# One number in a hybrid SSD and forgetting-attention layer: the last group's recurrence enters the stream of products one product later

## The chip, the cores and the metric

The kernel runs on one core of a Trainium2 chip. The metric is the device time of one execution in microseconds (us), given as the median of several runs. The core has five engines with a queue each: TensorE (PE in the profile, with its weight loads as PEld), VectorE (DVE), ScalarE (ACT), GpSimd (POOL) and SyncE (SP), which here only issues DMAs.

## The reference

One decoder layer over a sequence of 1024 tokens with 1024 channels, all in float32. A Mamba-2 branch (SSD) and a forgetting-attention branch share one input projection and are merged by gates:

```python
h = rmsnorm(x)
z_ssm, xbc, dt, q, k, v, f, z_att, g_ssm, g_att = split(h @ w_in)
xs, B, C = split(silu(causal_conv(xbc)))           # 16 heads of 64, 4 groups, state 128
dt = softplus(dt + dt_bias);  a = -exp(a_log)
# chunks of 128 tokens: inside a chunk  y = ((C B^T) * decay) (xs dt), between chunks a carried state
y_ssm = group_rmsnorm(ssd(xs, dt, a, B, C, d_skip) * silu(z_ssm))
# 16 attention heads of 64, logits q.k/8 + F[t] - F[s], F = cumsum(log sigmoid(f)), causal
y_att = attention(q, k, v, f) * silu(z_att)
merged = sigmoid(g_ssm) * (y_ssm @ w_branch_ssm) + sigmoid(g_att) * (y_att @ w_branch_att)
out = x + rmsnorm(merged @ w_out)
```

## The kernel before, in words

**Products.** All large projections are computed as pairs: two blocks of weight columns against the input, by a scheme of seven products of half-sized blocks instead of eight. A product has one operand made from the input (`x0` to `x6`, each split into a high part `x0h` and a low part `x0l`) and one made from the weights (`wop`, from a loaded piece `raw` or a `sum` of pieces). It is 12 matmuls of 128x512 (the helper in line 130), and it is run in two halves of 6. The weight operands are split by ScalarE (L354, the high part) and VectorE (L356, the low part; L363 and L379 make the sums). Products accumulate in the PSUM banks `pb`, `pc`, `pd`; VectorE and ScalarE take them out (L410, L418, L420, L422, L424), and what follows a finished projection (a tanh in L668, a product in L669, a store) stands right behind.

**The stream.** `Stream` holds one long list of products: for each of the four SSM groups first the pairs b and c, q, x, z, v, k; then the gates (`za`, `gs`, `ga`); then the two branch projections and the last one. `half()` runs the next half of a product, with the preparation of the third product behind it, and one entry of `chores` (small pieces of other work, such as those of `weights_work`, L243 and L244). `until(pair)` runs on to the end of a pair, and `beside(gen)` runs a generator that yields how many halves are to be run between its pieces. So the order of everything is written out: TensorE, and with it the other engines, meet the pieces of the recurrence and of the attention at fixed places among the products.

**The SSM part.** For each group: when its x pair is done, some halves run, and then the recurrence `ssd(g)` beside the stream: 8 chunks of 128 tokens. The conv of x (L803) and its SiLU (L810 on ScalarE, L811 on VectorE, which makes `xs`) come before. Per chunk: `sums` loads the cumulated decays, broadcast to all partitions (`csb`, L859, on SP's queue); `decays` makes the decay matrix `m` from them on ScalarE (L891 four times, L895); `first` turns `xs` and `bt` on TensorE into the bank `tr` (L133) and makes there the product of `ct` and `bt`; out of `tr` come `xdt` (L872, VectorE), `cbm` (L877, VectorE), `bn` (L880, ScalarE) and the masked `m` (L882, VectorE). `more` makes `xe` on GpSimd, `states` the matmul `st` from `bn` and `xe`, `second` the outputs `yps` from `m` and `xdt`. Its norm (`gate_and_norm`) runs beside the stream ahead of the next group's recurrence, after the last group ahead of the attention.

**The attention part.** Eight pairs of heads with six sets of scores each run beside the remaining products. A set is: `scores` (matmuls into four banks `s`, a custom sum and row minimum in L1526 on VectorE, the exponential in L1530 on ScalarE, both into `ex`), `turned` (TensorE turns `ex` into banks `pt`, which share the four buffers of `s`; ScalarE, and VectorE in L1548 for one bank of up to four, copy them to `p`), `weighted` (the matmul `av`). When a pair of heads has two of its six sets done, its row factors are settled (L1425, L1427, L1439 to L1444, VectorE), turned, stored by GpSimd's DMA (`st_dram`, L1454) and read back broadcast to all partitions as `rb` by SP's DMA (L1460); L1491 on VectorE multiplies the outputs by `rb`. `fill` shares the products that are left over all these pieces, with fixed weights.

## Time and profile before

| What | Value |
|---|---|
| median of 3 runs | 1295.31 us (1292.98 to 1297.67) |
| the profiled execution | 1294.79 us, of which the span is 1293.1 us |
| TensorE's granted clock, mean over the span | 0.997 |
| TensorE (PE) busy | 1253.8 us, 97%, 7066 instructions |
| its weight loads (PEld) | 986.1 us, 76%, beside the matmuls |
| VectorE (DVE) busy | 1014.7 us, 78% |
| ScalarE (ACT) busy | 794.3 us, 61% |
| GpSimd (POOL) busy | 284.6 us, 22% |
| DMA | 233.60 MB, HBM 182 GB/s over the span |

A row of the profile's timeline has the start in us from the span's start, the duration in us, the engine, the line, the operation, what is written from what, the shapes, and in square brackets the idle time ahead of it and what ended it. "128x512" is 128 partitions by 512 elements; `PE s L130 <- DVE p L1548` reads: TensorE's matmul into `s` waited for what VectorE did to `p` in line 1548. A row of a stretch has its window, its length, then for TensorE, its weight loads, VectorE, ScalarE and GpSimd the busy time with the count of instructions, TensorE's granted clock, and the DMA's share and GB/s.

### The profile page before, as it was taken

What the parts mean: (1) busy time and instruction counts of PE and PEld (TensorE: products, weight loads), DVE (VectorE), ACT (ScalarE), POOL (GpSimd) and SP (SyncE); (2) the same over time, 40 slices, a digit from 0 to 9 for tenths busy, and PEclk for the clock granted to TensorE, in tenths of its full rate; (3) what the DMA queues carried; (4) which work ended last, traced back from release to release, by engine and by line L of the source; (5) the groups of instructions that cost most, each with busy time, mean ns of one, the idle gap of its engine ahead of it and who ended that gap; (6) DMA issues with size and microseconds to landing.
All of it is one profiled execution on the core that took longest, in us unless ns stands there. A gap on an engine that the chain in (4) does not pass through costs nothing. (4 is left out here: it accounts for less than half of the span.)

```text
span 1293.1 us, 21078 instructions
## 1 busy us (share of the span) xinstructions
PE 1253.8 (97%) x7066; PEld 986.1 (76%) x7066; DVE 1014.7 (78%) x1979; ACT 794.3 (61%) x1728; POOL 284.6 (22%) x307
## 2 busy tenths in 40 slices
PE   6999999999999999899999999999999999999998
PEld 4787888788888888688776777777767777678786
DVE  6998888888789878788676766676789767876875
ACT  8755666466556756566555666566677556743654
POOL 0000330024102320143001222222121313256052
PEclk9999999999999999999999999999999999999999
DMA  7332543644363545445564657666677657665932
GB/s 281 104 106 71 154 148 121 199 140 146 127 210 116 153 153 164 122 154 154 168 237 153 221 175 224 193 208 196 228 282 250 219 178 253 230 219 189 364 112 102
DMA packets 154669, 233.60 MB, mean 181 GB/s; under 512 B 17216, under 2 KB 62656, under 8 KB 154560
## 3 DMA queue, kind: packets, MB, share of 16 engines
q1 hardware_dynamic: 142016, 205.53, 49.8%
q0 software_dynamic: 6400, 16.10, 3.3%
q10 hardware_dynamic: 6144, 10.62, 2.2%
q8 instruction: 56, 0.92, 0.3%
q14 instruction: 53, 0.43, 0.1%
HBM read 162.99 MB, written 72.34 MB: 182 GB/s over the span
## 5 line engine op out<-in xcount | busy, mean ns | idle before, releaser
L356 DVE TENSOR_TENSOR wop<-sum,wop 128x512 fp32r<-128x512 f32 x174 | 140.5, 808 | 53.4 <-ACT wop L354 52.7
L354 ACT ACTIVATE wop<-sum 128x512 fp32r<-128x512 f32 x174 | 108.8, 626 | 99.0 <-DVE sum L363 44.7
L1530 ACT ACTIVATE ex<-ex,nm 128x512 f32<-128x512 f32 (+1 forms) x192 | 116.1, 606 | 76.9 <-DVE nm L1526 75.7
L410 ACT ACTIVATE s<-pb 128x512 f32<-128x512 f32 x141 | 83.5, 592 | 97.3 <-PE pb L130 95.9
L130 PE MATMUL pc<-x3h,wop 128*128 128x512 f32 x384 | 131.6, 399 | 2.5 <-ACT wop L354 2.0
L130 PE MATMUL pb<-x0h,wop 128*128 128x512 f32 x384 | 132.2, 400 | 0.7 <-ACT x0h L1246 0.6
L130 PE MATMUL pc<-x2h,wop 128*128 128x512 f32 x384 | 131.4, 399 | 0.4 <-DVE u L422 0.4
L130 PE MATMUL pb<-x6h,wop 128*128 128x512 f32 x376 | 129.2, 399 | 1.6 <-ACT s L410 1.6
L130 PE MATMUL pb<-x5h,wop 128*128 128x512 f32 x376 | 128.3, 398 | 1.3 <-ACT s L410 1.3
L130 PE MATMUL pb<-x4h,wop 128*128 128x512 f32 x376 | 128.6, 398 | 0.2 <-DVE wop L356 0.2
L356 DVE TENSOR_TENSOR wop<-raw,wop 128x512 fp32r<-128x512 f32 x149 | 104.3, 702 | 29.8 <-ACT wop L354 29.5
L1526 DVE CUSTOM_DVE_ANT_0 ex<-s,fb 128x512 f32<-128x512 f32 (+1 forms) x192 | 96.8, 553 | 24.4 <-PE s L130 24.3
L354 ACT ACTIVATE wop<-raw 128x512 fp32r<-128x512 f32 x151 | 93.8, 623 | 15.8 <-PE pc L130 10.1
L130 PE MATMUL pd<-x1h,wop 128*128 128x512 f32 x264 | 89.1, 396 | 0.0
L130 PEld LDWEIGHTS pc<-x3h,wop 128*128 128x128 f32 x384 | 72.1, 188 | 20.2 <-issue 3.8
L130 PEld LDWEIGHTS pb<-x0h,wop 128*128 128x128 f32 x384 | 72.5, 189 | 17.2 <-ACT x0h L1246 1.3
L130 PEld LDWEIGHTS pc<-x2h,wop 128*128 128x128 f32 x384 | 72.1, 188 | 16.1 <-DVE u L422 0.8
L130 PEld LDWEIGHTS pb<-x6h,wop 128*128 128x128 f32 x376 | 70.6, 188 | 18.1 <-ACT s L410 2.7
L130 PEld LDWEIGHTS pb<-x5h,wop 128*128 128x128 f32 x376 | 70.6, 188 | 17.5 <-ACT s L410 2.2
L130 PEld LDWEIGHTS pb<-x4h,wop 128*128 128x128 f32 x376 | 70.5, 188 | 15.7 <-issue 0.7
L130 PE MATMUL s<-k,q 64*128 64x512 f32 (+3 forms) x576 | 75.7, 373 | 6.2 <-DVE p L1548 4.4
L214 POOL TENSOR_TENSOR wd<-wd 128x256 f32<-128x256 f32 x32 | 31.3, 978 | 228.3 <-DMA wd<-in_wo 125.7
(341 smaller groups left out, 3012.1 us busy)
## 6 DMA issues: line engine op xcount, KB each, us to landing
raw<-in_wu SPq DMA_DIRECT2D x128, 256.0 KB, 3.7
csb<-cs_dram SPq DMA_DIRECT2D x32, 256.0 KB, 5.5
fb<-f_dram SPq DMA_DIRECT2D x16, 512.0 KB, 6.5
rb<-st_dram SPq DMA_DIRECT2D x48, 128.0 KB, 3.2
wd<-in_wo SPq DMA_DIRECT2D x40, 128.0 KB, 3.1
xt<-in_x SPq DMA_DIRECT2D x8, 512.0 KB, 5.8
gs_dram<-th ACTq DMA_DIRECT2D x16, 256.0 KB, 3.4
qh_dram<-th SPq DMA_DIRECT2D x16, 256.0 KB, 5.2
```

The source lines that it names most:

```text
L130: return tc.keep_in_program_order(nc.tensor.matmul(*args, **kw))
L214: pin(nc.gpsimd.tensor_tensor(t[out_], t[a_], t[b_], ALU.subtract))
L354: nc.scalar.activation(op[:, 0], src, AF.Copy, scale=sign)
L356: nc.vector.tensor_tensor(op[:, 1], src, op[:, 0], ALU.subtract)
L410: nc.scalar.activation(s, ps, AF.Copy)
L1526: nc.vector.tensor_tensor_reduce(o, s[e][:, 0:w], fb[hp, h][:, e, 0:w], 1.0, 3.0e38, ALU.add, ALU.min, nm)
L1530: pin(nc.scalar.activation(o, o, AF.Exp, scale=-1.0, bias=nm, accum_out=hd.at(hd.sm, i, h, e)))
```

## The change

```diff
@@ the loop over the four SSM groups
             stream.beside(norm)
             stream.until(by_group[g][2])
-            stream.halves(4)
+            stream.halves(4 if g < 3 else 6)
             if g == 0:
                 stream.chores += list(weights_work())
             stream.beside(ssd(g))
             norm = gate_and_norm(g)
```

Between the end of the x pair of group 3 and its recurrence three products stand instead of two. The instructions are the same in number on every engine; the order is the same up to this place. Behind it all pieces of the last recurrence, of its norm and of the attention up to the last pair of heads stand one product later among the products. The pieces of the last pair of heads have two halves of products less between them, since the list of products ends where it did.

TensorE, where the last group's recurrence begins (`tr` is the bank into which the first chunk is turned, `pb<-x5h` the end of the last product of pair z, `pb<-x0h` the first product of pair v, `pb<-x6h` the second). Before:

```order
L130 MATMUL pb<-x5h,wop 128x512
L133 MATMUL tr<-ident,xs_5243 128x128
L133 MATMUL tr<-ident,xs_5350 128x128
L133 MATMUL tr<-ident,bt 128x128
L130 MATMUL tr<-ct,bt 128x128
L130 MATMUL pb<-x0h,wop 128x512
```

Now:

```order
L130 MATMUL pb<-x0h,wop 128x512
L133 MATMUL tr<-ident,xs_5243 128x128
L133 MATMUL tr<-ident,xs_5350 128x128
L133 MATMUL tr<-ident,bt 128x128
L130 MATMUL tr<-ct,bt 128x128
L130 MATMUL pb<-x6h,wop 128x512
```

The whole product of `x0` (12 matmuls) now stands ahead of the turning instead of behind it.

ScalarE at the same place, from the tanh of the SiLU (L810) to the copy of `bn` and the decay matrices (`m_5514` is that of the second chunk, whose first has been made further up; `m_5492` is that of the first). Before:

```order
L810 ACTIVATE th<-xs_5243 128x512
L410 ACTIVATE s<-pb 128x512
L354 ACTIVATE wop<-raw 128x512
L668 ACTIVATE th<-th 128x512
L880 ACTIVATE bn<-tr 128x128
L891 ACTIVATE m_5514<-csb,cscol 128x128 x4
L668 ACTIVATE th<-th 128x512
```

Now:

```order
L810 ACTIVATE th<-xs_5243 128x512
L410 ACTIVATE s<-pb 128x512
L354 ACTIVATE wop<-raw 128x512
L668 ACTIVATE th<-th 128x512 x2
L410 ACTIVATE s<-pb 128x512
L243 ACTIVATE wl<-wd 128x256
L891 ACTIVATE m_5492<-csb,cscol 128x128 x4
L354 ACTIVATE wop<-sum 128x512
L880 ACTIVATE bn<-tr 128x128
```

`bn` stood behind one tanh of L668; it now stands behind both, an L410, an L243, the four L891 of the first chunk and an L354.

VectorE at the same place, from the SiLU to `xdt` and `cbm`. Before:

```order
L811 SCALAR_TENSOR_TENSOR xs_5350<-th,xs_5350 128x512 x2
L420 TENSOR_TENSOR th<-pd,s 128x512
L356 TENSOR_TENSOR wop<-sum,wop 128x512
L811 SCALAR_TENSOR_TENSOR xs_5243<-th,xs_5243 128x512
L872 TENSOR_TENSOR xdt<-tr,dtn 128x256
L877 TENSOR_TENSOR cbm<-tr,tri 128x128
L422 TENSOR_TENSOR th<-pc,s 128x512
```

Now:

```order
L811 SCALAR_TENSOR_TENSOR xs_5350<-th,xs_5350 128x512 x2
L356 TENSOR_TENSOR wop<-sum,wop 128x512
L420 TENSOR_TENSOR th<-pd,s 128x512
L811 SCALAR_TENSOR_TENSOR xs_5243<-th,xs_5243 128x512
L363 TENSOR_TENSOR sum<-sum,raw 128x512
L422 TENSOR_TENSOR th<-pc,s 128x512
L356 TENSOR_TENSOR wop<-raw,wop 128x512
L669 SCALAR_TENSOR_TENSOR th<-th 128x512
L872 TENSOR_TENSOR xdt<-tr,dtn 128x256
L877 TENSOR_TENSOR cbm<-tr,tri 128x128
```

Four operations for the products (`sum`, L422, `wop`, L669) now stand ahead of `xdt` and `cbm`.

VectorE in the first pair of heads, behind the multiplication by `rb` (L1491, two rows ahead of the first one here), up to the copy of `p`. Before:

```order
L1427 TENSOR_TENSOR dd<-nr,nm 128x4 x2
L422 TENSOR_TENSOR th<-pc,s 128x512
L356 TENSOR_TENSOR wop<-sum,wop 128x512
L1439 TENSOR_TENSOR sm<-sm,dd 128x8
L379 TENSOR_TENSOR sum<-sum,raw 128x512
L669 SCALAR_TENSOR_TENSOR th<-th 128x512
L1440 TENSOR_TENSOR sm<-sm 128x4
L1441 RECIPROCAL sm<-sm 128x4
L1444 SCALAR_TENSOR_TENSOR ns<-dd,sm 128x8
L1548 COPY p<-pt 128x512
```

Now:

```order
L1427 TENSOR_TENSOR dd<-nr,nm 128x4 x2
L356 TENSOR_TENSOR wop<-raw,wop 128x512
L1439 TENSOR_TENSOR sm<-sm,dd 128x8
L1440 TENSOR_TENSOR sm<-sm 128x4
L1441 RECIPROCAL sm<-sm 128x4
L1444 SCALAR_TENSOR_TENSOR ns<-dd,sm 128x8
L1548 COPY p<-pt 128x512
```

Three operations of 128x512 (L422, L379, L669) no longer stand between L1491 and the copy of `p`.

On SP's queue the third load of `csb` stood ahead of the second of two loads of `raw`, a store of `t_w`, two stores of the gate z (`zg_dram`, L670) and a store of `t_low`; it now stands behind them.

## The prediction: what the later entry does to the time

> **What bounds the kernel now.** I read the page's busy times first, then TensorE's waits by line, then the timelines of TensorE, VectorE and ScalarE around the last group's entry, and then the same three engines wherever TensorE waited long in the attention part behind it.

> ```profile
> PE 1253.8 (97%) x7066; PEld 986.1 (76%) x7066; DVE 1014.7 (78%) x1979; ACT 794.3 (61%) x1728; POOL 284.6 (22%) x307
> ...
> PE s L130 <- DVE p L1548: 4.4, 4, 3.2
> PE tr L133 <- DVE xs L811: 2.5, 1, 2.5
> PE pc L130 <- ACT wop L354: 2.0, 1, 2.0
> ```

> TensorE is the bound: busy 97% of the span, and its instructions are the same 7066 after the change, in another order. So the time moves only by TensorE's waits, and by any change of its clock. Three long ones count here: 3.2 us before a set of scores (`s`), 2.5 us before the turning (`tr`) of the values, 2.0 us before a product into `pc`. The second is the one the change touches. It is in the last group:

> ```profile
> 540.53 0.39 PE L130 MATMUL pb<-x5h,wop 128*128 128x512 f32 x1
> 540.76 0.27 PE L133 MATMUL tr<-ident,xs 128*128 128x128 f32 x1
> 543.54 0.33 PE L133 MATMUL tr<-ident,xs 128*128 128x128 f32 x1 [2.51 <-DVE xs L811]
> ...
> 543.96 0.48 PE L130 MATMUL pb<-x0h,wop 128*128 128x512 f32 x1
> ...
> 548.14 0.59 PE L130 MATMUL st<-xe,bn 128*128 128x256 f32 x2
> ...
> 550.06 0.66 PE L130 MATMUL yps<-m,xdt 128*64 128x128 f32 x8
> ...
> 1148.98 2.72 PE pb L130 x12
> ```

> TensorE stands at the turning from 540.76 to 543.54, because VectorE has not finished the SiLU (L811). From there to the `st` and `yps` of the first chunk it runs without a wait. A whole product of twelve matmuls takes 2.72 us, a half 1.36 us.

> **The change part by part: the turning's wait.** Nothing is added or removed. The recurrence and the norm of group 3 (8 chunks with their matmuls, their VectorE, ScalarE and GpSimd work, 8 `csb` loads and the loads and stores of the norm on SP's queue) stand one product later. The product `pb<-x0` now runs at 540.76, where its weights are ready (it started without a wait at 543.96, and its operand was made from a `raw` piece ahead of the SiLU). It ends at 543.48; the turning is released at 543.54. So the 2.5 us of waiting are filled: **-2.5 us**. The 2.0 us wait into `pc` (535 us) lies ahead of the place where the orders part and stays.

> **What is late next.** VectorE does not get faster by this: TensorE merely arrives earlier at the next results.

> ```profile
> 542.27 1.82 DVE L811 SCALAR_TENSOR_TENSOR xs<-th,xs 128x512 f32<-128x512 f32 x2
> 544.01 0.68 DVE L420 TENSOR_TENSOR th<-pd,s 128x512 f32<-128x512 f32 x1
> 544.61 0.68 DVE L356 TENSOR_TENSOR wop<-sum,wop 128x512 fp32r<-128x512 f32 x1
> 545.21 0.68 DVE L811 SCALAR_TENSOR_TENSOR xs<-th,xs 128x512 f32<-128x512 f32 x1
> 545.81 0.41 DVE L872 TENSOR_TENSOR xdt<-tr,dtn 128x256 f32<-128x256 f32 x1
> ...
> 546.34 0.68 DVE L422 TENSOR_TENSOR th<-pc,s 128x512 f32<-128x512 f32 x1
> ...
> 548.75 0.68 DVE L882 TENSOR_TENSOR m<-m,cbm 128x512 f32<-128x512 f32 x1
> ```
> ```profile
> 546.52 0.28 ACT L880 ACTIVATE bn<-tr 128x128 f32<-128x128 f32 x1 [1.10 <-DVE cbm L877]
> 546.69 1.27 ACT L891 ACTIVATE m<-csb,cscol 128x128 f32<-128x128 f32 x4
> 547.87 0.62 ACT L668 ACTIVATE th<-th 128x512 f32<-128x512 f32 x1
> 548.39 0.40 ACT L243 ACTIVATE wl<-wd 128x256 fp32r<-128x256 f32 x1
> 548.69 0.58 ACT L410 ACTIVATE s<-pb 128x512 f32<-128x512 f32 x1
> 549.17 0.62 ACT L354 ACTIVATE wop<-sum 128x512 fp32r<-128x512 f32 x1
> 549.69 0.62 ACT L895 ACTIVATE m<-m 128x512 f32<-128x512 f32 x1
> ...
> csb<-cs_dram SPq DMA_DIRECT2D x32, 256.0 KB, 5.5
> ```

> I walk through the new order with these starts (on VectorE a 512-wide operation each 0.60 us: 544.01, 544.61, 545.21). VectorE, free of the two SiLU operations at 544.01, does `wop`, `th` (L420), the third SiLU, `sum`, and then L422, which runs 546.41 to 547.09. TensorE: turning 543.54 to 543.96, product `pb<-x6` to 546.68, and then `pc<-x2`, which adds onto the bank that L422 reads: it waits 0.4 us. After half a product (548.45) comes `st`, which needs `bn`. On ScalarE `bn` now stands behind the second L668, which needs L422's result: 547.1 + 0.52 (L668) + 0.48 (L410) + 0.30 (L243) + 1.18 (four L891) + 0.52 (L354) = 550.1, and 0.28 for `bn` itself: `st` starts at 550.4, **a wait of 1.9 us**. Behind it half a product and `st` end at 552.0. `yps` needs `m`: four more L891 (551.4), L895 (552.0), then L882 on VectorE (552.7): 0.7 us. Together 0.4 + 1.9 + 0.7 = **+3.0 us** where no wait stood before. So the local sum is +0.5 us: the wait changes its place. Bounds: -2.5 us if none of the three appears (before the change none did), and +2 us, since the third `csb` load now stands on SP's queue behind stores that wait for VectorE until about 550 us; with 5.5 us to landing it comes at about 555.5, and its four L891 (558.09 before) then end just in time for the next `st`; a late landing would add about 1.5 us. GpSimd's `xe` only follows `xdt`, ahead of `bn`, and is not what `st` waits for.

> **The attention part.** It keeps its halves between the pieces up to the last head, but each piece meets other products. The longest wait of all lies in the first head:

> ```profile
> 701.93 0.39 PE L130 MATMUL pb<-x6h,wop 128*128 128x512 f32 x1
> 705.52 1.65 PE L130 MATMUL s<-k,q 64*128 64x512 f32 x6 [3.21 <-DVE p L1548]
> ...
> 708.64 2.08 PE L130 MATMUL av<-p,v 128*64 128x256 f32 x16
> ...
> 1074.70 0.98 PE L130 MATMUL s<-k,q 64*128 64x512 f32 x6
> ...
> 1076.44 0.87 PE L130 MATMUL av<-p,v 128*64 128x256 f32 x8
> ```
> ```profile
> 700.55 0.69 DVE L1491 TENSOR_TENSOR o<-o,rb 128x512 f32<-128x512 f32 x1 [4.37 <-DMA rb<-st_dram]
> ...
> 701.77 0.68 DVE L422 TENSOR_TENSOR th<-pc,s 128x512 f32<-128x512 f32 x1
> ...
> 703.09 0.69 DVE L379 TENSOR_TENSOR sum<-sum,raw 128x512 f32<-128x512 f32 x1
> 703.69 0.69 DVE L669 SCALAR_TENSOR_TENSOR th<-th 128x512 f32<-128x512 f32 x1
> ...
> 704.78 0.68 DVE L1548 COPY p<-pt 128x512 f32<-128x512 f32 x1
> ...
> 705.60:708.90 3.30, 3.30 (x22) 2.17 (x24) 1.92 (x6) 0.75 (x4) 0.00 (x0) 0.50 0.09 35
> ```

> VectorE stands 4.37 us at L1491 for the load of `rb`; the copy of `p` that frees the scores' bank comes 4.23 us behind that. In the new order L422, L379 and L669 stand ahead of L1491, where VectorE was idle, and only the rest is left behind it: 3 x 0.60 = 1.8 us less, the copy ends at 703.7 and TensorE, free at 702.3, waits 1.4 us. ScalarE's copies of the other banks can add some tenths; I take 1.6 us, so -1.6. The last row adds something: in the 3.3 us behind that wait TensorE's granted clock was 0.50. The same shape of scores took 3.12 us here (705.52 to 708.64) and 1.74 us in the last head (1074.70 to 1076.44): 1.4 us more. If the wait shrinks to 1.6 us I expect no such stretch, since behind the 2.51 us wait the products ran on at full pace. **-3.0 us** in all. Bounds: 0, if `rb` lands that much later, and -4.6, if `rb`, with fewer loads in front, lands 1.5 us earlier and nothing is waited for.

> [...]

> In the last head two halves of products go (there is one product less left to fill with), one of them ahead of the turning of the fourth set:

> ```profile
> 1108.54 0.71 ACT L1530 ACTIVATE ex<-ex,nm 128x512 f32<-128x512 f32 x1
> ...
> 1111.64 1.64 PE L133 MATMUL pt<-ident,ex 128*128 128x128 f32 x13 [0.38 <-ACT ex L1530]
> ```

> With 1.36 us less cover the 0.38 us wait would grow to 1.7. But the exponentials (L1530) started only at 1108.54 because two splits of `x1` ahead of them on ScalarE waited for loads; in the new order those splits stand behind. I take 0, with bounds of -0.4 and +1.4. The other waits in the attention part are single ones of at most 1.2 us; other products beside them make some longer and some shorter. I take 0, and plus or minus 2 us. The sum: -2.5 + 3.0 - 3.0 + 0 + 0 = **-2.5 us**. The profiled execution took 1294.79 us, 0.5 below the median of 1295.31; the forecast goes against the median: **1292.8 us**.

> **The rivals.** (1) *The turning's wait simply goes.* For it: none of the three new waits is seen before, and the trace runs from 543.54 to the next `yps` without one. Against it: VectorE's queue is full from 542.27 to 549, and `bn` stands behind a result of that queue. Then -2.5 - 3.0 = -5.5: 1289.8 us, faster by 0.4%. (2) *A long wait at half clock elsewhere.* Each head has the step at L1491; with other products around, a later head may get the three operations between `rb` and the copy of `p`, and a wait above 3 us there costs 3.2 + 1.4 = 4.6 us. With the first head's wait kept, which the same late load would do, it is +0.5 + 4.6 = +5.1: 1300.4 us, slower. It decides once the wait there passes about 3.2 us. For it: the load of `rb` comes late wherever big loads stand in front; against it: of 8 heads one shows it. (3) *Nothing moves:* the wait goes to `st`, and the first head still waits for `rb`: +0.5 us, 1295.8 us.

> **How the numbers follow.** A measurement of this kernel tells about 0.3% (3.9 us; the three runs spread over 4.7 us) from no change: below 1291.4 is faster, above 1299.2 slower. The forecast 0.42, rival (1) 0.28, (2) 0.10, (3) 0.20. The forecast's own spread (2 us either way) puts 0.05 of it below 1291.4, and 0.02 of (3) above 1299.2: faster 0.33, same 0.55, slower 0.12. The range goes from 1288.5 (rival 1 with the load early) to 1297.5 (rival 3 with the late `csb` or the last head's 1.4 us).

> **What would show it.** In the profile after: no wait at the first `tr` of the last group, and one of about 2 us at the first `st`, ended by ScalarE's `bn`. In the first head, a wait of 1 to 2 us at the fourth set of scores, and no window with a granted clock of 0.5 before the end. The prediction is wrong if `st` does not wait, or if a wait above 3 us stands anywhere in the attention part.

## The result: slower by 0.4%, and the profile after

| | kernel before | changed kernel |
|---|---|---|
| median | 1295.33 us (13 runs, 1292.22 to 1299.25) | 1301.18 us (13 runs, 1295.63 to 1306.34) |
| ratio | | 1.0042, 95% interval 1.0030 to 1.0054 |
| profiled execution | 1294.79 us, span 1293.1 | 1301.18 us, span 1299.0 |

The forecast of 1292.8 us was wrong, and the range (to 1297.5) did not hold the time. A gain was forecast, a loss was measured.

The page of the changed kernel, its busy line and TensorE's longest waits by line (what waited, for what, us in total, times, longest):

```profile
PE 1255.0 (97%) x7066; PEld 987.6 (76%) x7066; DVE 1017.7 (78%) x1979; ACT 795.6 (61%) x1728; POOL 287.3 (22%) x307
...
PE s L130 <- DVE p L1548: 5.7, 6, 3.4
PE st L130 <- POOL xe L904: 2.5, 2, 1.8
PE st L130 <- ACT bn L880: 1.7, 1, 1.7
PE tp L133 <- DVE ns L1444: 1.7, 1, 1.7
PE pc L130 <- DVE th L420: 1.7, 1, 1.7
```

The wait for the SiLU (`tr`, 2.5 us) is gone from the list, and waits for `bn`, `xe`, `ns` and `th` have come that the kernel before did not have in this size. The timeline of TensorE shows the places:

```profile
543.35 0.39 PE L130 MATMUL pb<-x0h,wop 128*128 128x512 f32 x1
543.58 0.47 PE L133 MATMUL tr<-ident,xs 128*128 128x128 f32 x2
...
550.71 0.67 PE L130 MATMUL st<-xe,bn 128*128 128x256 f32 x2 [1.74 <-ACT bn L880]
...
593.43 0.48 PE L130 MATMUL st<-xe,bn 128*128 128x256 f32 x1 [1.77 <-POOL xe L904]
...
708.18 0.50 PE L130 MATMUL s<-k,q 64*128 64x512 f32 x2
...
965.89 0.62 PE L130 MATMUL s<-k,q 64*128 64x384 f32 x4 [3.35 <-DVE p L1548]
```

The first turning starts at 543.58 without a wait, the scores at 708.18, where the kernel before lost 3.21 us, too. But `st` waits in the first chunk and again in the sixth (593.43), and the longest wait is now in the sixth pair of heads (965.89).

Where the time went, from the starts of TensorE's rows in two profiled executions of each kernel (the second ones are the runs e3_again and f3_before_again below). The parts end at the last `tr` of the third and of the fourth group's recurrence, and at the first `s` of a pair of heads. Where a product has changed its part (2.72 us), the last column takes it out.

| Part | before, two profiles | changed, two profiles | mean difference |
|---|---|---|---|
| up to the third group's last `tr` | 457.87, 457.72 | 458.55, 457.89 | +0.4 |
| last group's recurrence | 140.66, 141.23 | 146.07, 146.09 | +2.4 |
| its norm, up to the first scores | 64.44, 64.69 | 63.72, 63.72 | -0.8 |
| first pair of heads | 62.80, 60.01 | 58.52, 59.00 | -2.6 |
| second to fifth | 229.25, 229.07 | 234.37, 230.49 | +3.3 |
| sixth | 62.53, 63.25 | 63.60, 64.01 | +0.9 |
| seventh | 57.15, 57.50 | 58.65, 58.25 | +1.1 |
| last pair and all behind it, up to TensorE's last row | 211.60, 211.62 | 208.73, 209.04 | 0.0 |

The sum is +4.7 us, the difference of the mean spans (1297.15 and 1292.5). Two of its parts lean on one execution. Of the +2.4 us of the recurrence, 0.9 lies ahead of its first `tr`, where e3 alone ran 3.4 us at half clock (granted clock 0.51), behind the wait into `pc` that the prediction put at 535 us. And the second to fifth pair of heads stand 5.2 us above the kernel before in the first profile, but 1.3 us in e3.

The medians lie further apart (5.9 us) than these profiles, which were both taken at a mean granted clock of 0.997. Of the 19 executions of the changed kernel (13 here, 6 in e3) nine had a mean clock of 0.993 or 0.994 and took 1302.2 us in the mean; the other ten, at 0.996 and 0.997, took 1298.9. The 12 executions of f3 all had 0.996 to 0.998 and took 1294.2. So about 1.6 of the 6.3 us between the means of the two kernels goes with more time at half clock; this is an estimate from these means.

### The profile page after: what moved, and what is told of

Its sections match the earlier page's. It is cut to its first block, busy times and chain, and to the rows that moved or that the text cites. A ratio compares the mean times of both kernels' runs of the same rounds, so it can differ in the third digit from the quotient of the medians.

```text
span 1299.0 us, 21079 instructions
## 1 busy us (share of the span) xinstructions
PE 1255.0 (97%) x7066; PEld 987.6 (76%) x7066; DVE 1017.7 (78%) x1979; ACT 795.6 (61%) x1728; POOL 287.3 (22%) x307
## 5 line engine op out<-in xcount | busy, mean ns | idle before, releaser
L356 DVE TENSOR_TENSOR wop<-sum,wop 128x512 fp32r<-128x512 f32 x174 | 138.8, 799 | 54.7 <-ACT wop L354 54.2
L354 ACT ACTIVATE wop<-sum 128x512 fp32r<-128x512 f32 x174 | 108.9, 627 | 95.3 <-DVE sum L363 39.1
L1530 ACT ACTIVATE ex<-ex,nm 128x512 f32<-128x512 f32 (+1 forms) x192 | 116.3, 607 | 68.6 <-DVE nm L1526 67.8
L410 ACT ACTIVATE s<-pb 128x512 f32<-128x512 f32 x141 | 83.7, 594 | 101.5 <-PE pb L130 98.4
L130 PE MATMUL pc<-x3h,wop 128*128 128x512 f32 x384 | 131.5, 399 | 4.5 <-ACT wop L354 2.0
L130 PE MATMUL pb<-x0h,wop 128*128 128x512 f32 x384 | 133.1, 401 | 0.7 <-ACT x0h L1246 0.6
L130 PE MATMUL pc<-x2h,wop 128*128 128x512 f32 x384 | 132.3, 400 | 0.0
L130 PE MATMUL pb<-x6h,wop 128*128 128x512 f32 x376 | 128.6, 398 | 1.8 <-ACT s L410 1.8
L130 PE MATMUL pb<-x5h,wop 128*128 128x512 f32 x376 | 128.4, 398 | 1.3 <-ACT s L410 1.3
L130 PE MATMUL pb<-x4h,wop 128*128 128x512 f32 x376 | 127.7, 397 | 0.3 <-DVE wop L356 0.3
L356 DVE TENSOR_TENSOR wop<-raw,wop 128x512 fp32r<-128x512 f32 x149 | 108.5, 730 | 20.8 <-ACT wop L354 20.0
L1526 DVE CUSTOM_DVE_ANT_0 ex<-s,fb 128x512 f32<-128x512 f32 (+1 forms) x192 | 96.9, 553 | 29.1 <-PE s L130 29.0
L354 ACT ACTIVATE wop<-raw 128x512 fp32r<-128x512 f32 x151 | 93.9, 624 | 15.5 <-PE pc L130 11.6
L130 PE MATMUL pd<-x1h,wop 128*128 128x512 f32 x264 | 89.3, 396 | 0.0
L130 PEld LDWEIGHTS pc<-x3h,wop 128*128 128x128 f32 x384 | 72.1, 188 | 22.1 <-ACT wop L354 3.0
L130 PEld LDWEIGHTS pb<-x0h,wop 128*128 128x128 f32 x384 | 72.6, 189 | 17.3 <-ACT x0h L1246 1.7
L130 PEld LDWEIGHTS pb<-x6h,wop 128*128 128x128 f32 x376 | 70.7, 188 | 18.2 <-ACT s L410 2.9
L130 PEld LDWEIGHTS pc<-x2h,wop 128*128 128x128 f32 x384 | 72.1, 188 | 16.0 <-issue 0.7
L130 PEld LDWEIGHTS pb<-x5h,wop 128*128 128x128 f32 x376 | 70.6, 188 | 17.4 <-ACT s L410 2.2
L130 PE MATMUL s<-k,q 64*128 64x512 f32 (+3 forms) x576 | 76.3, 369 | 7.4 <-DVE p L1548 5.7
L130 PEld LDWEIGHTS pb<-x4h,wop 128*128 128x128 f32 x376 | 70.4, 188 | 16.0 <-DVE wop L356 0.9
## 6 DMA issues: line engine op xcount, KB each, us to landing
raw<-in_wu SPq DMA_DIRECT2D x128, 256.0 KB, 3.9
csb<-cs_dram SPq DMA_DIRECT2D x32, 256.0 KB, 5.5
gs_dram<-th ACTq DMA_DIRECT2D x16, 256.0 KB, 3.6
qh_dram<-th SPq DMA_DIRECT2D x16, 256.0 KB, 5.0
```

The lines of the kernel that those rows point to most:

```text
L130: return tc.keep_in_program_order(nc.tensor.matmul(*args, **kw))
L354: nc.scalar.activation(op[:, 0], src, AF.Copy, scale=sign)
L356: nc.vector.tensor_tensor(op[:, 1], src, op[:, 0], ALU.subtract)
L410: nc.scalar.activation(s, ps, AF.Copy)
L1526: nc.vector.tensor_tensor_reduce(o, s[e][:, 0:w], fb[hp, h][:, e, 0:w], 1.0, 3.0e38, ALU.add, ALU.min, nm)
L1530: pin(nc.scalar.activation(o, o, AF.Exp, scale=-1.0, bias=nm, accum_out=hd.at(hd.sm, i, h, e)))
```

## The experiments

All ratios are to the kernel before, with 95% intervals.

**The parts of the shift.** e1 moves the recurrence and leaves the attention where it was, e2 the reverse. e3 is the changed kernel once more, f3 the kernel before.

```diff
 e1, on the changed kernel           e2, on the kernel before
-        for _ in range(14):         -        for _ in range(14):
+        for _ in range(12):         +        for _ in range(16):
             stream.half()                        stream.half()
```

> The recurrence and norm of group 3 stand one product later, the attention where it stood before (12 halves instead of 14 ahead of the first scores). Theory A (two costs that add up: waits inside the recurrence, read from the two traces as +2.6 us, and another set of meetings in the attention, +3.3 us): 2.6 us over before, ratio 1.002, with the first head's wait of about 3 us back. Theory B (it is all in the recurrence, and the attention only differs from one execution to the next): ratio 1.004. Theory C (all in the attention): ratio 1.000.

> The recurrence stands where it stood before, the attention one product later (16 halves instead of 14). Theory A: 3.3 us over before, ratio 1.0025, the wait of 2.5 us at the first turning kept, none of over 1 us at st, and the waits of the changed kernel in the attention (1.7 us in the second head, 3.3 us at half clock in the sixth). Theory B: ratio 1.000. Theory C: ratio 1.004.

> The changed kernel once more, for a second profiled execution. Theory A: the waits stand at the same places with the same sizes within 0.5 us (1.7 us at the first st, 1.7 us at the sixth chunk's st, 1.7 us in the second head, 3.3 us in the sixth with 3.4 us at half clock behind it). Rival: the wait in the sixth head lies near the edge of the half clock and is below 3 us in this execution; then this profile is 1.5 to 2 us shorter. Ratio 1.004 either way.

> The kernel before once more, for a second profile: the wait at the first turning of the last group (2.5 us) and the one in the first head (3.2 us) at the same places within 0.5 us, and st without a wait of over 0.3 us in the last group. From the profiles so far I expect stretches of half clock of 3.41 us or twice that only behind 3.41 us in which TensorE was idle for about 1.9 us or more, so that the waits of 2 to 3 us here cost 1.4 us more in one execution and nothing more in another. Ratio 1.000.

e1: 1.0041 (1.0025 to 1.0058). e2: 1.0016 (1.0000 to 1.0032). e3: 1.0043 (1.0026 to 1.0059). f3: 1.0003 (0.9993 to 1.0013). In e3 the waits stand at the same places but not all in the same size: 0.83 us at the first `st`, 1.75 at the sixth chunk's, 3.95 in the sixth pair, none of over 0.6 in the second. f3's two long ones, in the timeline of TensorE:

```profile
542.33 0.33 PE L133 MATMUL tr<-ident,xs 128*128 128x128 f32 x1 [2.76 <-DVE xs L811]
...
704.96 0.50 PE L130 MATMUL s<-k,q 64*128 64x512 f32 x2 [1.98 <-DVE p L1548]
```

The second was 3.21 us in the first profile: 1.2 us less, against the expectation. By the ratios alone theory B seemed right: the recurrence alone costs as much as the whole change. The run was repeated later, for a second profile:

> The recurrence alone one product later once more, for a second profile and a narrower interval: ratio 1.003 to 1.005. The waits at st (1.7, 0.9 and 1.4 us in its first profile) stand again; if the waits of 1.8 and 1.3 us in the first head (at 677 and 680 us, with 6.8 us at half clock) stand again too, they belong to it; if not, they were those of one execution, and the ratio is nearer to 1.002.

g4: 1.0054 (1.0041 to 1.0066), just above the range expected. Its waits at `st` are 1.73, 0.66 and 0.76 us (1.74, 0.86 and 1.38 in e1). Its VectorE and TensorE in the first pair of heads:

```profile
666.75 0.69 DVE L363 TENSOR_TENSOR sum<-raw 128x512 f32<-128x512 f32 x1 [3.05 <-DMA raw<-in_wu]
...
672.27 0.33 PE L133 MATMUL pt<-ident,ex 128*128 128x128 f32 x1 [2.08 <-ACT ex L1530]
...
675.18 0.47 PE L133 MATMUL pt<-ident,ex 128*128 128x128 f32 x1 [1.21 <-ACT ex L1530]
...
673.70:680.50 6.80, 5.59 (x20) 4.30 (x22) 2.19 (x4) 3.53 (x9) 0.00 (x0) 0.50 0.45 150
```

VectorE stands 3.05 us for a load of `raw`, the sums of the scores (L1526) queue behind it, the exponentials and the turning come late, and 6.8 us at half clock follow (the last row, a stretch with its granted clock ahead of the last two columns). The same two waits of TensorE stand in e1's profile (1.78 and 1.27 us). The changed kernel has none of this: its attention stands two halves further behind the norm. So e1's loss is in good part one of its own, and theory B falls. The change cannot be taken apart into two halves that add up: each alignment of pieces and products has waits of its own. e2 alone shows the changed attention's waits (3.04 us in the sixth pair, none of over 0.6 in the second), the turning's wait (2.87 us), no wait at `st`, and a smaller loss.

**Is it the recurrence's `st`?** f1 lets `st` stand half a product later in the changed kernel, f2 does it to the kernel before, g2 to e1.

```diff
 in ssd(g), each chunk (and the same shift ahead of the first)
             decays(c + 2)
-            yield 1
+            yield 1 + (g == 3)
             if c + 1 < NT:
                 prev, new = states(c + 1, new)
-            yield 1
+            yield 1 - (g == 3)
```

> The changed kernel, and in group 3 the matmul st stands half a product later in every chunk, right ahead of yps (as many halves per chunk as before). Theory R (the loss is made in the recurrence by st waiting for bn and for xe: 1.74, 0.77 and 1.77 us in the first profile of the changed kernel): each of the three shrinks by up to 1.36 us, 3 to 4 us less, ratio to before 1.001. Rival S (the recurrence only delays what follows; its own waits are not the loss): the three waits shrink, the time stays at 1.004. Rival T (yps then waits instead, for m or for the state): waits of the same size at yps, 1.004.

> The same edit on the kernel before, as a control: there st waits nowhere by more than 0.2 us in the profile. Theory R: nothing to gain, ratio 1.000. If st standing later is good or bad by itself, it shows here by the same amount as in the changed kernel.

> The recurrence alone one product later (attention as in the kernel before), and st half a product later in group 3. If the waits at st are the whole loss of the recurrence, this is as fast as the kernel before: ratio 1.000 (0.999 to 1.001). If the recurrence loses elsewhere too, in what it leaves behind for the attention, the ratio stays at 1.002 or more.

f1: 1.0022 (1.0009 to 1.0035). f2: 1.0002 (0.9990 to 1.0014). g2: 1.0054 (1.0036 to 1.0071). In f1's profile `st` waits 0.38 us in the first chunk and nowhere else by over 0.3; a part came back in the first chunk at `yps`, as rival T had it:

```profile
551.53 0.67 PE L130 MATMUL st<-xe,bn 128*128 128x256 f32 x2 [0.38 <-ACT bn L880]
553.85 0.66 PE L130 MATMUL yps<-m,xdt 128*64 128x128 f32 x8 [1.65 <-DVE m L882]
```

The recurrence took 143.28 us instead of 146.07 and 146.09; counted from its first `tr`, which leaves out the half clock of e3 ahead of it, it took 3.0 and 1.3 us less. The ratio fell by 0.0020, which is 2.6 us, less than the 3 to 4 us expected: theory R holds for this part, and the edit is worth nothing where `st` does not wait (f2). g2 missed its expectation: its recurrence took 142.46 us instead of e1's 146.39, but the waits in the first pair of heads stayed (1.70 and 1.12 us), and the time with them.

**Is it the attention's sixth pair?** e4 makes `rb` land earlier, by storing the row factors from ScalarE's queue. g3 and h1 take away nearly all of GpSimd's work at the place (two subtractions, 512 columns cut to 8), in the changed kernel and in the one before. h4 does the subtractions in full on VectorE.

```diff
 e4 (L1453; the two stores also move under the copy's high_priority)
-                    pin(nc.gpsimd.dma_start(st_dram[...], st[...]))
+                    nc.scalar.dma_start(st_dram[...], st[...])
 g3, h1 (L1593 and L1594; n8 is slice(0, 8) but for the last pair of heads)
-                pin(eng.tensor_tensor(x, zr, x, ALU.subtract))
-                pin(eng.tensor_tensor(y, x, y, ALU.subtract))
+                pin(eng.tensor_tensor(x[:, n8], zr[:, n8], x[:, n8], ALU.subtract))
+                pin(eng.tensor_tensor(y[:, n8], x[:, n8], y[:, n8], ALU.subtract))
 h4
-            eng = nc.vector if hp == NK - 1 else nc.gpsimd
+            eng = nc.vector if h or hp == NK - 1 else nc.gpsimd
```

> The changed kernel with the stores of the row factors (L1454) issued by ScalarE, right behind the copy that makes them, instead of by GpSimd. Theory D (the waits in the second and sixth heads come from the late landing of rb): VectorE's waits at L1491 shrink by a median of 1 us or more, the 1.7 us and the 3.3 us of TensorE with the half clock go, 4 to 6 us faster than the changed kernel, ratio to before 1.000. Rival E (GpSimd's two subtractions of L1593 and L1594 slow VectorE in the sixth head, and the landing of rb does not decide): the sixth head keeps a wait of over 2 us, ratio 1.003.

> The changed kernel with GpSimd's two subtractions for the fifth to seventh head pair (L1593, L1594) cut from 512 to 8 columns; the rest of those two operands is left out, the order of every engine is the same. Theory E (GpSimd's work slows VectorE's operations beside it: 2.2 us instead of 0.69 for the second L279 and 1.23 instead of 0.2 for L1436): both take their usual time, TensorE's wait in the sixth head (3.35 us, 3.95 us in the two profiles) is 2.5 us smaller and no half clock follows it; 2 to 4 us less, ratio to before 1.001 to 1.003. Rival D (only the landing of rb decides): the wait stays above 2.5 us, ratio 1.004.

> The kernel before with GpSimd's two subtractions for the fifth to seventh head pair cut from 512 to 8 columns (the rest of those operands is left out), order unchanged. If GpSimd's work costs only where the new order put a scores' bank behind it, nothing is won here: ratio 0.999 to 1.000, since no wait in the sixth head pair of this kernel is over 1.3 us. If it is a gain of any order, 3 to 5 us less: ratio 0.997.

> The changed kernel with the two subtractions on VectorE instead of GpSimd (nothing left out). Theory E: the copy of p ahead of the scores of the sixth head pair no longer stands behind slowed operations, TensorE's wait there falls below 1.5 us with no half clock, 2 to 4 us less than the changed kernel: ratio to before 1.001 to 1.002. Rival: VectorE's added 1.4 us take the place of the slowed ones, the wait stays above 2.5 us, 1.004.

e4: 1.0065 (1.0044 to 1.0086). VectorE's waits at L1491 shrank from 17.7 us in total (10 waits) to 5.0 (4 waits), the 1.7 us in the second pair went, and yet the time grew: the sixth pair's wait stayed (4.00 us, and the eight `av` matmuls behind it took 1.55 us, where they took 0.87 in g3), and with ScalarE's order changed by the issues another of 1.82 us stood in the same pair. Theory D falls as an account of the loss.

The place in the changed kernel, VectorE and GpSimd:

```profile
959.34 0.69 DVE L1491 TENSOR_TENSOR o<-o,rb 128x512 f32<-128x512 f32 x1 [1.55 <-DMA rb<-st_dram]
...
960.95 2.82 DVE L279 SCALAR_TENSOR_TENSOR x4l<-x4l,x4h 128x512 fp32r<-128x512 f32 x2
963.69 1.23 DVE L1436 TENSOR_SCALAR ns<-sm 128x8 f32<-128x8 f32 x1
964.83 0.68 DVE L422 TENSOR_TENSOR th<-pc,s 128x512 f32<-128x512 f32 x1
965.43 0.41 DVE L1548 COPY p<-pt 128x256 f32<-128x256 f32 x1
...
961.93 1.28 POOL L1593 TENSOR_TENSOR x<-zr,x 128x512 f32<-128x512 f32 x1
963.29 1.60 POOL L1594 TENSOR_TENSOR y<-x,y 128x512 f32<-128x512 f32 x1
```

and in g3, with the same order:

```profile
955.57 0.69 DVE L1491 TENSOR_TENSOR o<-o,rb 128x512 f32<-128x512 f32 x1 [1.33 <-DMA rb<-st_dram]
...
957.18 1.29 DVE L279 SCALAR_TENSOR_TENSOR x4l<-x4l,x4h 128x512 fp32r<-128x512 f32 x2
958.40 0.17 DVE L1436 TENSOR_SCALAR ns<-sm 128x8 f32<-128x8 f32 x1
958.48 0.68 DVE L422 TENSOR_TENSOR th<-pc,s 128x512 f32<-128x512 f32 x1
959.08 0.41 DVE L1548 COPY p<-pt 128x256 f32<-128x256 f32 x1
...
959.54 0.79 PE L130 MATMUL s<-k,q 64*128 64x384 f32 x5 [0.55 <-DVE p L1548]
```

From L1491 to the copy of `p`, which frees the scores' bank, 6.09 us pass beside GpSimd's full subtractions and 3.51 us without them: the two L279 took 2.82 us instead of 1.29, and the tiny L1436 took 1.23 instead of 0.17. This is not one execution's accident: the stretch took 6.05 to 6.11 us in all five profiles with this order and the full subtractions (the changed kernel, e2, e3, e4, f1), 3.50 and 3.51 us in the two with the cut (g3, i1). TensorE's wait there went from 3.35 to 0.55 us. g3: 1.0004 (0.9992 to 1.0015), so 4.9 us less than the changed kernel. h1: 1.0002 (0.9991 to 1.0014): the kernel before wins nothing by the same cut. It has the slowed L279, too (1.92 us, across L1593), but no set of scores waits by more than 0.3 us in its sixth pair. Theory E holds: the slowed operations cost time in the new order and none in the old.

That g3 is as fast as the kernel before does not mean that this place was the whole loss. Its sixth pair of heads took 60.45 us: 3.2 and 3.6 us less than in the changed kernel, but also 2.1 and 2.8 us less than in the kernel before. So by this profile the new order would have won time in this pair, and GpSimd's work turned that into a loss of 0.9 us (in i1 below, where `rb` came later, the pair took 62.61 us). g3's second to fifth pair (231.2 us) stays slower than in the kernel before: its time is a balance of a gain here with losses elsewhere.

The operation in the kernel before and in the changed one (shortest, median and longest, ns, ahead of the first and last start):

```profile
L279 DVE SCALAR_TENSOR_TENSOR x4l<-x4l,x4h x11: 681/685/1916, 949.2 to 1210.8; 128x512 fp32r<-128x512 f32 x11
```
```profile
L279 DVE SCALAR_TENSOR_TENSOR x4l<-x4l,x4h x11: 683/685/2215, 952.2 to 1216.7; 128x512 fp32r<-128x512 f32 x11
```

The rows put GpSimd beside the slow ones. The second operation of L279 took 2.2 us instead of 0.69, across L1593 (961.93 to 963.21), and L1436 took 1.23 us instead of 0.17 while L1594 ran (963.29 to 964.89). In g3, with L1593 at 0.38 us and L1594 at 0.20, the two L279 took 1.29 us together and L1436 0.17. By what way GpSimd's work slows VectorE's, no run shows.

h4: 1.0038 (1.0023 to 1.0053). The scores' wait fell to 1.24 us as theory E had it, but the time did not follow. TensorE's two rows behind it:

```profile
959.16 0.79 PE L130 MATMUL s<-k,q 64*128 64x384 f32 x5 [1.24 <-DVE p L1548]
...
963.99 0.38 PE L133 MATMUL tp<-ident,ns 128*8 128x128 f32 x1 [3.11 <-DVE nm L1526]
```

With the subtractions on VectorE its order is another: the copy of `p` stands ahead of the two L279, and these stand with L1594 and two L282 between the copy and the next L1526, which starts 4.54 us behind the copy instead of 1.65. `tp`, which takes a bank that L1526 reads, waits 3.11 us: a wait turned into the next one. Since the copy no longer stands behind L279 at all, h4 does not test theory E by itself; g3 and h1 do.

**Both places at once.** i1 is f1 with the subtractions cut as in g3.

> The changed kernel with st half a product later in group 3 and with GpSimd's two subtractions for the fifth to seventh head pair cut to 8 columns (the rest of those operands is left out): both places of the loss taken away at once. Alone the first won 2.6 us (1.0042 to 1.0022), the second 4.9 us (to 1.0004). If they are two separate losses, together 7.5 us: ratio to before 0.998 to 0.999. If the second only moves waits that the first also frees, 1.000 or above.

i1: 1.0000 (0.9984 to 1.0015). The expected 0.998 to 0.999 lies within the interval, but so does the value of g3 alone, so it is not shown that the two losses add up. In its profile `rb` came later (VectorE waited 3.23 us at L1491), and the sixth pair waited 2.44 us though nothing slowed VectorE:

```profile
953.70 0.69 DVE L1491 TENSOR_TENSOR o<-o,rb 128x512 f32<-128x512 f32 x1 [3.23 <-DMA rb<-st_dram]
...
957.67 0.62 PE L130 MATMUL s<-k,q 64*128 64x384 f32 x4 [2.44 <-DVE p L1548]
```

The 3.51 us from L1491 to the copy are the same as in g3. So the wait there has two shares: when `rb` lands, which differs from execution to execution (VectorE waited 1.55 us for it in the first profile of the changed kernel, 2.17 in e3), and 2.6 us for GpSimd.

**How late, or beside what?** f4 moves the recurrence two products, with the attention in its old place; h2 repeats it, g1 adds f1's edit, h3 adds h4's.

```diff
-            stream.halves(4 if g < 3 else 6)
+            stream.halves(4 if g < 3 else 8)
...
-        for _ in range(14):
+        for _ in range(10):
```

> The recurrence of group 3 two products later than in the kernel before (8 halves instead of 4), the attention where it stood before (10 halves instead of 14). Theory U (what counts is which products the chunks meet, not how late they stand): a loss unlike that of one product, between 0 and 4 us, ratio 1.000 to 1.003, with waits at other chunks. Rival V (the later, the worse: pieces crowd behind): twice the loss of the recurrence alone, ratio 1.007 to 1.008.

> The recurrence two products later, attention as in the kernel before, once more. If the gain is real: ratio 0.997 to 0.9995, again with waits of about 2 us at st in the third chunk and none of over 1 us between 672 and 690 us. If it was the draw of the half clock in those executions: 1.000 or above.

> Two products later, st half a product later in group 3, the attention as in the kernel before: the two edits that each won something, together. If what is left of waits in the recurrence two products later (0.81 us for bn and 2.07 us for xe with 3.4 us at half clock behind it) goes as it went one product later, 2 to 4 us less than two products later alone: ratio to before 0.996. If yps waits in its place, 0.998 as without it.

> The same with the two subtractions on VectorE instead of GpSimd (nothing left out). VectorE takes 2 x 0.69 us more per head pair but is not slowed beside GpSimd. If that helps in any order: 0.995 to 0.997; if only in the order of the changed kernel, as two products later alone, 0.998 to 1.000.

f4: 0.9981 (0.9966 to 0.9996). h2: 0.9990 (0.9979 to 1.0002). g1: 1.0005 (0.9990 to 1.0020). h3: 1.0000 (0.9987 to 1.0013). Later is not worse: rival V falls. A gain was not in theory U's range (1.000 to 1.003) either, though its longest wait at `st` does stand at another chunk. Two products are better than one (e1, g4) by 0.5%. The gain over the kernel before is 0.1 to 0.2%, and the interval excludes no change in one run of the two; the spans of the profiles (1293.3 and 1292.1) do not show where it would come from, and that stays open. A part may be the draw of the half clock, which is not shown: the mean granted clock was 0.9978 over f4's executions and 0.9968 over h2's, 0.9971 and 0.9969 over those of the kernel before beside them. No wait of over 1 us stands between 672 and 690 us, but one at `st` does, by the same chain as in the changed kernel, VectorE waiting 5.10 us for `raw` ahead of `xdt`:

```profile
565.34 0.69 DVE L363 TENSOR_TENSOR sum<-raw 128x512 f32<-128x512 f32 x1 [5.10 <-DMA raw<-in_wu]
...
570.37 0.48 PE L130 MATMUL st<-xe,bn 128*128 128x256 f32 x1 [2.07 <-POOL xe L904]
```

g1's edit did not take it away (2.09 us), and its time missed both values that were expected (0.996 and 0.998). h3 has the second of its two values: the subtractions on VectorE win nothing in this order. Of the kernels that leave nothing out, only this one (f4, h2) measured faster than both the kernel before and the changed one.

## Why the prediction was wrong, step by step

*The turning's wait.* Right: filled, and the turning starts at 543.58, as forecast.

*The new waits behind it, +3.0.* For `st` the walk was near: 1.9 us forecast, 1.74 measured in the first profile, but 0.83 in e3, ended by `bn` at this place:

```profile
550.31 0.26 ACT L880 ACTIVATE bn<-tr 128x128 f32<-128x128 f32 x1
```

At `pc` and `yps` less than forecast came (none of over 0.3 us, and 0.27). For `yps` the walk was too long by its own rows: half a product and `st` take 1.92 us in the view before (548.14 to 550.06), where it used 1.6, so its 0.7 us would have been 0.4. What failed is where the walk stopped: after the first chunk. "GpSimd's `xe` only follows `xdt`, ahead of `bn`, and is not what `st` waits for" is wrong in the third chunk (0.77 us) and in the sixth (1.77, in e3 1.75):

```profile
589.28 0.69 DVE L363 TENSOR_TENSOR sum<-raw 128x512 f32<-128x512 f32 x1 [3.03 <-DMA raw<-in_wu]
...
591.69 0.42 DVE L872 TENSOR_TENSOR xdt<-tr,dtn 128x256 f32<-128x256 f32 x1
...
592.19 1.19 POOL L904 TENSOR_TENSOR xe<-xdt,tend 128x256 f32<-128x256 f32 x1 [6.82 <-DVE xdt L872]
```

A `sum` whose `raw` lands late now stands on VectorE ahead of `xdt`, and `xe` itself took 1.19 us here, where its median is 0.62. The local sum of +0.5 us (bounds to +2) was +2.4 in the recurrence, -0.8 in the norm behind it; without the 0.9 us ahead of the first `tr` about +0.7. So its size was near, by luck: less came in the first chunk than forecast, waits that the walk had excluded came in later ones, and the norm, which it did not price, gave time back. The late third `csb` ended no wait of TensorE.

*The first head, -3.0.* The size was near, 2.6 us in the mean (4.3 between the first profiles, 1.0 between the second ones), but the forecast's path made only a part of it. It left a wait of 1.6 us; the wait is gone altogether. The multiplication by `rb` in the changed kernel:

```profile
703.24 0.69 DVE L1491 TENSOR_TENSOR o<-o,rb 128x512 f32<-128x512 f32 x1 [1.39 <-DMA rb<-st_dram]
```

The copy of `p` starts at 706.04, 2.80 us later (3.22 in e3), where it was 4.23 in both profiles before: 1.4 and 1.0 us less, where 1.8 was forecast. The rest is an earlier `rb`. L1491 starts 34.91 and 34.97 us behind the pair's first scores, before it was 37.58 and 36.34; the forecast had that among its bounds only. Some 0.7 us of the mean is a draw, too: the half clock behind this wait, 1.4 us by the prediction's rows, stood in the first profile before and not in f3, whose wait was 1.98 us. The price of 1.4 us for the half clock was near (1.74 below); what brings it on was not understood: rival (2) put it at a wait of about 3.2 us, and in the runs 1.95 us were enough where they fell within one stretch (below).

*The last head, 0.* Right: 0.0, as a sum; waits of 1.2 us at `s` and 1.7 at `tp` came in it and others went.

*The other attention waits, 0 plus or minus 2.* This is the term that failed: +5.3 us (second to fifth pair 3.3, sixth 0.9, seventh 1.1). By execution it is 7.2 us in the first, 3.4 in e3 and 4.6 in f1, whose attention has the same order, so it is outside the 2 us each time. Rival (2) had its main place, a head with a late `rb` and then operations ahead of the copy of `p`, and half clock behind. It got a chance of 0.10, because it was sought by counting waits in the old order ("of 8 heads one shows it"), while the VectorE rows of the new order around each L1491 could have been walked as the first head's were. What neither it nor the sum had is GpSimd's share, though a slowed L279 (1.92 us) stands in the trace before, where it cost nothing. What makes the 1.1 us of the seventh pair, and the 1.3 to 5.2 us of the second to fifth, no run tested; that stays open.

Between the forecast's -2.5 us and the +4.7 us of the profiles lie 7.2 us: 5.3 in the heads that were not walked, 1.1 in the recurrence and its norm (0.9 of it ahead of the first `tr`), 0.4 in the first head, and 0.4 ahead of the change, where the orders are the same. The sum was made from the two places that were walked through, with 0 and a symmetric 2 us for six pairs of heads that were not.

Of the signs that the prediction named, two came: no wait at the first `tr`, and one of about 2 us at `st`, ended by `bn`. Two did not: the wait of 1 to 2 us in the first head, and the absence of half clock (0.50 from 967.40 to 970.80 us). Its sign of being wrong, a wait above 3 us in the attention part, stood in the sixth pair. One of its sums does not come out of its own terms, though nothing hangs on it: rival (1) with the load early is 1288.2 us, not 1288.5.

## What to carry to other kernels

When a change shifts a long train of pieces against another, the place it was made for is one of many meetings. Walk every meeting where an engine's queue holds something that waits for a DMA, with what TensorE needs queued behind it, or price the unwalked ones by their number and not by zero. Look also for rows that are slow in the trace before at no cost (here a VectorE operation of 1.9 us that takes 0.7 elsewhere): a new order can put the critical path behind them.

## What the runs showed of the hardware

The half clock hung on where a wait fell, not only on its length. The same wait at the same matmul in two executions of the changed kernel, with the stretch behind it (granted clock ahead of the last two columns), the first execution and then e3:

```profile
535.33 0.47 PE L130 MATMUL pc<-x3h,wop 128*128 128x512 f32 x1 [2.05 <-ACT wop L354]
...
535.30:538.70 3.40, 3.37 (x15) 2.85 (x16) 3.40 (x7) 2.26 (x5) 0.00 (x0) 1.00 0.20 61
```
```profile
534.75 0.47 PE L130 MATMUL pc<-x3h,wop 128*128 128x512 f32 x1 [2.03 <-ACT wop L354]
...
535.70:539.10 3.40, 3.40 (x9) 2.66 (x9) 3.40 (x6) 1.54 (x4) 0.00 (x0) 0.51 0.53 160
```
